# One tile as home of biases, residual, one-hots and split scores, and another first stage, in a hybrid conv, attention and PEER step

## The chip, the cores and the metric

The kernel runs on one core of one Trainium2 chip. The metric is the device time of one execution in microseconds. The kernel before took 1293.79 us in the median of three runs (1292.43 to 1293.86). The profiled execution took 1293.86 us; its span, from the first to the last recorded instruction, is 1292.1 us.

## The reference, cut to what matters

One layer over 256 prompt rows and 32 sample rows (8 sequences of 4), model width 1024, all in fp32:

```
h  = rmsnorm(x) * g1
p  = h @ w_in                        # 76 column tiles of 128: conv, q, k, v, gates
yA = w_out_a(B * conv3(C * hc))
yB = w_out_b(attention(q, k, v))     # 3 windows x 8 head slots, distance biases
x  = x + w_o(sigmoid(ga) * yA + sigmoid(gb) * yB)
h2 = rmsnorm(x) * g2
q  = h2 @ peer_wq                    # product keys, top 16 of 16 x 16
x  = x + sum over 16 experts of gate * gelu(h2 . u[e]) * v[e]
y  = rmsnorm(x) * gfin
```

The outputs are y and the updated key, value and convolution buffers. For the prompt rows all 16384 experts are computed densely and gated by one-hot products; for the 32 sample rows the chosen experts are gathered. The updated caches are mostly copies of the old ones, 56 transfers from DRAM to DRAM, most of them 1 MB.

## The kernel before, in words

The weights are 368 blocks of 128 x 1024 (`wpack`), each 0.52 MB. SP's queue loads them in order into four buffers `raw`; ACT rounds each to a high half `whi` (line 102), VectorE or, for the blocks in `pool_lo`, GpSimd subtracts for the low half `wlo` (line 103). Three splits stand ahead of the block in use. A block with eight k tiles takes 24 matmuls: high by high, high by low and low by high (`mm3`, lines 116 to 120). The blocks in order are q (0 to 11), k (12 to 23), v, conv (36 to 59), w_out_a with gate A, w_out_b with gate B (76 to 87), w_o (88 to 95), peer_wq (96 to 111), U (112 to 239) and V (240 to 367).

Every engine runs its instructions in the order in which the program writes them. A generator scheduler (`Flow`) steps attention and normalisation pieces in between the blocks of the projections. Waits are put in by the framework: an instruction waits for what wrote the parts that it reads, and a tile of a new pool waits for the tiles of the closed pools before it.

**First stage (lines 195 to 241).** Eight constant matmuls (`heat`, line 222). SP's queue gets the first slice of x transposed (`xf`, four slices of 0.29 MB), then raw0, then the other slices, then raw1 and so on. ACT's queue gets g1 and x in its natural layout (`xt`, 1.18 MB). ACT and VectorE split `xf` times g1 into `uxH` and `uxL`, eight slices of 128 x 288 (lines 232 and 233); behind slice 3 the split of block 1 stands in both queues. Blocks 0 to 2 have their low halves from GpSimd. Block 0's matmuls with the low weights come behind its others (lines 279 to 283). Three squares of `xt` on ACT give the row sums, `rstd` the reciprocal root (a dozen small operations), and three products with the identity a diagonal, which a matmul with ones spreads over the partitions behind block 3 (line 509): q is computed from unnormalised x and scaled afterwards.

**Biases.** `biasS` and `biasP` are loaded on POOL's queue behind the first stage (lines 254 and 255), with the convolution's weights and state and two K chunks behind them. The sample and prompt scores read them.

**w_o (lines 695 to 735).** Behind gate B the program issues six of the cache copies on SP (line 688), splits the first w_o block, closes the attention pools and opens new ones. POOL's queue then loads x transposed again (`x2T`, 1.18 MB, line 702), `g2T` (4 KB), `g2n` (0.52 MB) and `iotaR` (64 KB). For each of eight column tiles c: 24 matmuls into one of two accumulators, then on VectorE

```
V.tensor_add(x2T[:, c, :], x2T[:, c, :], o[:, :NT])
...
S.activation(u2H[:, c, :], x2T[:, c, :], AF.Copy, scale=g2T[:, c:c + 1])
```

then the low half `u2L`, a square on ACT and its addition to `ssum`. ACT's split of a coming weight block stands between two rounds. On SP's queue the loads of block 94 and later stand behind the six copies.

**U stage (lines 1024 to 1053).** 128 blocks of scores with gelu. In between, 64 steps build one-hot tiles `hot` and weighted ones `wgt` (lines 980 to 988, both 128 x 1024 in fp16, three buffers each), whose matmuls give the dense gates. `ev` (two buffers) holds gelus on their way to be gated.

**V stage (lines 1058 to 1080).** 128 blocks; for each pair of experts `split_w` makes high and low halves `ah` and `al` of the gated scores (128 x 512, two buffers each), a pair ahead of the matmuls. Then the final norm.

Of the kernel before, what the change touches and what calls it, by code (L numbers as in the profile page):

```python
# [19 lines left out]
P = 128  # L20
# [46 lines left out]
def emit(ctx, tc, a):  # L67
# [19 lines left out]
    pool_lo = {0, 1, 2} | set(range(B_WQ + 5, B_U + 48, 2))  # L87
# [102 lines left out]
    x2d = a["x2_spill"]  # L190
    ca = ExitStack()
    pa = ca.enter_context(tc.tile_pool(name="pa", bufs=1, side="right"))
    if True:
        with ExitStack() as c1:
            hH = p2.tile([P, KT, NT], F32R, tag="hi", name="hH")
            hL = p2.tile([P, KT, NT], F32R, tag="lo", name="hL")
            uxH = pa.tile([P, KT, 384], F32R, tag="hi", name="uxH")[:, :, :NT]
            uxL = pa.tile([P, KT, 384], F32R, tag="lo", name="uxL")[:, :, :NT]
            ss = cp.tile([P, 3], F32, name="n1s")
            with tc.tile_pool(name="pn1", bufs=1) as pn:  # L200
                xf = pn.tile([P, KT, NT], F32, name="xf")
                xt = pn.tile([P, 3, D], F32, name="xt")
                sq = pn.tile([P, D], F32, name="sq")
                g1T = pn.tile([P, KT], F32, name="g1T")
                warm = pn.tile([P, P], F32, name="warm")
                V.memset(warm, 1.0)
                V.memset(ss, 1.0)
                S.dma_start(g1T, a["g1T"])
# [5 lines left out]
                G.dma_start(cst, a["consts"][:, 128:177])  # L214
                G.dma_start(ident, a["consts"][:, 0:128])
# [3 lines left out]
                load_to(RAW)  # L219
                S.activation(ss[:1, 0:1], warm[:1, 0:1], AF.Sqrt)  # L220
                heat = bg.get()
                for _ in range(8):
                    T.matmul(heat[:, :P], warm, warm, start=True, stop=True)
                bg.put()

                def square(t):
                    w = NS if t == 2 else P
                    S.activation(sq[:w], xt[:w, t, :], AF.Square, accum_out=ss[:w, t:t + 1])

                split_next()  # L230
                for k in range(KT):
                    S.activation(uxH[:, k, :], xf[:, k, :], AF.Copy, scale=g1T[:, k:k + 1])
                    V.scalar_tensor_tensor(uxL[:, k, :], xf[:, k, :], g1T[:, k:k + 1], uxH[:, k, :].bitcast(F32),
                                           op0=OP.mult, op1=OP.subtract)
                    if k == 3:
                        split_next()
                split_next()
# [11 lines left out]
            biasP = p1.tile([P, 1152], F32, tag="bp", name="biasP")  # L249
            biasS = p1.tile([P, 1088], F32, tag="bs", name="biasS")  # L250
            convw = p1.tile([P, 8, 3], F32, name="convw")
            stT = p1.tile([P, 8, 8, 2], F32, name="stT")
            cvo = p1.tile([P, 8, 18], F32, name="cvo")
            G.dma_start(biasS, a["biasS"])
# [35 lines left out]
            def kv_load(n):  # L290
                while kv_n[0] < min(n, 28):
                    i = kv_n[0]
                    st, ch = divmod(i % 14, 7)
                    if i < 14 and i % 4 >= 2:
                        kvt[i] = pa.tile([P, 3072], F32, tag=("hi", "lo")[i % 2], name=f"kv{i}")[:, :2048]
# [183 lines left out]
            ones = p1.tile([P, P], F32, name="ones")  # L479
            rrow = wk.tile([P, NT], F32, tag="t", name="rrow", bufs=5)  # L480
            V.memset(ones, 1.0)
            for t in range(3):
                w = P if t < 2 else NS
                V.tensor_scalar_mul(diag[:w, t * P:t * P + w], ident[:w, :w], rs[:w, t:t + 1])
# [105 lines left out]
            zH = pa.tile([P, KT, 384], F32R, tag="hi", name="zH")[:, :, :NT]  # L590
            zL = pa.tile([P, KT, 384], F32R, tag="lo", name="zL")[:, :, :NT]
# [63 lines left out]
            flow.drain()  # L655

            mixH = pa.tile([P, KT, 384], F32R, tag="hi", name="mixH")[:, :, :NT]
            mixL = pa.tile([P, KT, 384], F32R, tag="lo", name="mixL")[:, :, :NT]
# [42 lines left out]
    x2T = pt2.tile([P, KT, NT], F32, name="x2T")  # L701
    G.dma_start(x2T, a["xT"])
# [240 lines left out]
    def run_s(i):  # L943
# [6 lines left out]
        if g:  # L950
            e = oh.tile([P, NP], F32, tag="ev", name=f"ev{i}", bufs=2)
# [26 lines left out]
    def gates():  # L978
        def hot(u):
            e = oh.tile([P, 2, 2, P, 2], F16, tag="hot", name=f"hot{u}", bufs=3)  # L980
# [316 lines left out]
```

## Time and profile before

| | |
|---|---|
| runs | 1292.43, 1293.79, 1293.86 us |
| profiled execution | 1293.86 us, span 1292.1 us |
| TensorE busy | 1232.3 us, 95% of the span |
| VectorE busy | 936.6 us, 72% |
| ACT busy | 592.3 us, 46% |
| GpSimd busy | 155.2 us, 12% |
| granted TensorE clock, mean | 0.983 of full |

Busy shares are means over stages with different limits, so the place where TensorE stands still is what one looks for. A wait is put down to the event that came last. Packets are what one DMA engine moved at a time; each transfer is spread over 16 engines, and each engine ends its part with a small packet that counts up a semaphore.

### The profile page before, as it was taken

To read this page: it belongs to the slowest core of one execution; us is meant where nothing else is said; L and a number is where in the kernel's file an instruction comes from. 1 tells how busy PE (TensorE), PEld (TensorE's weight loads), DVE (VectorE), ACT (ScalarE), POOL (GpSimd) and SP (SyncE) were. 2 spreads that over 40 slices of the span, in tenths; PEclk is the share of its full clock that TensorE was granted. 3 is DMA by queue.
4 is the path that set the end of the run, shared out by engine and by line. 5 is a ranking of instruction groups with operands and counts; after the bars stand their busy time and mean duration, and the time that the engine had idled before them with its cause. 6 is when DMAs were issued, how large, how long until landed. Compare 5 with 4: busy or idle time off the path is not lost.

```text
span 1292.1 us, 22943 instructions
## 1 busy us (share of the span) xinstructions
PE 1232.3 (95%) x9110; PEld 1126.9 (87%) x9110; DVE 936.6 (72%) x1720; ACT 592.3 (46%) x976; POOL 155.2 (12%) x110
## 2 busy tenths in 40 slices
PE   6999999999995799999999999999999999999996
PEld 6989998888995799989999999999988888888884
DVE  4745366764553565998997889899778877878875
ACT  4433443333352455544535444444455555555553
POOL 3000000000000022354400000000111111111100
PEclk7999999999998899999999999999999999999998
DMA  8587766566447567768767777675778888888872
GB/s 306 189 303 289 244 231 228 183 231 218 137 163 273 199 238 275 278 214 285 268 231 274 255 282 283 240 258 196 240 267 320 298 301 317 290 303 307 302 257 108
DMA packets 68235, 325.65 MB, mean 252 GB/s; under 512 B 8560, under 2 KB 8720, under 8 KB 59168
## 3 DMA queue, kind: packets, MB, share of 16 engines
q1 hardware_dynamic: 55984, 249.46, 55.5%
q0 software_dynamic: 9600, 67.19, 13.9%
q10 hardware_dynamic: 2544, 7.55, 1.5%
q8 instruction: 71, 1.16, 0.3%
q14 instruction: 36, 0.29, 0.1%
HBM read 318.19 MB, written 60.10 MB: 293 GB/s over the span
## 4 chain that ended last, share of the span: by engine, by line
PE 85%; DVE 7%; ACT 3%; DMA 3%; issue 2%; POOL 0%; DVEq 0%; SPq 0%; ACTq 0%
PE wide L1079 26%; PE acc L118 17%; PE acc L119 16%; PE acc L120 16%; DVE wlo L103 2%; PE wide L1002 2%; DMA iotaR<-iotaR 2%; ACT whi L102 2%; PE bg L356 1%; PE bg L325 1%; PE bg L444 1%; DVE tp_eq L854 1%; PE bg L390 1%; PE bg L346 1%; DVE qbd L376 1%
## 5 line engine op out<-in xcount | busy, mean ns | idle before, releaser
L103 DVE TENSOR_TENSOR wlo<-raw,whi 128x1024 fp32r<-128x1024 f32 x335 | 413.6, 1235 | 240.3 <-ACT whi L102 238.4
L102 ACT CAST whi<-raw 128x1024 fp32r<-128x1024 f32 x368 | 386.3, 1050 | 186.5 <-PE wide L1079 158.5
L120 PE MATMUL acc<-h2H,wlo 128*128 128x256 f32 x1024 | 289.4, 283 | 4.3 <-DVE wlo L103 4.0
L118 PE MATMUL acc<-h2H,whi 128*128 128x256 f32 x1024 | 292.9, 286 | 0.0
L119 PE MATMUL acc<-h2L,whi 128*128 128x256 f32 x1024 | 291.0, 284 | 0.0
L120 PEld LDWEIGHTS acc<-h2H,wlo 128*128 128x128 f32 x1024 | 193.1, 189 | 4.9 <-DVE wlo L103 4.4
L118 PEld LDWEIGHTS acc<-h2H,whi 128*128 128x128 f32 x1024 | 195.5, 191 | 0.2 <-issue 0.2
L119 PEld LDWEIGHTS acc<-h2L,whi 128*128 128x128 f32 x1024 | 194.7, 190 | 0.0
L118 PE MATMUL acc<-hH,whi 128*128 128x288 f32 x512 | 157.3, 307 | 1.9 <-ACT hH L494 1.1
L1079 PE MATMUL wide<-whi,ah 128*128 128x512 f32 x504 | 155.4, 390 | 1.6 <-ACT ah L1066 1.6
L1079 PE MATMUL wide<-wlo,ah 128*128 128x512 f32 x504 | 155.3, 389 | 0.0
L1079 PE MATMUL wide<-whi,al 128*128 128x512 f32 x504 | 155.1, 389 | 0.0
L120 PE MATMUL acc<-hH,wlo 128*128 128x288 f32 x512 | 150.8, 294 | 1.5 <-DVE wlo L103 1.5
L119 PE MATMUL acc<-hL,whi 128*128 128x288 f32 x512 | 151.2, 295 | 0.4 <-DVE hL L496 0.4
L1079 PEld LDWEIGHTS wide<-whi,ah 128*128 128x128 f32 x504 | 94.4, 188 | 22.1 <-ACT ah L1066 2.7
L1079 PEld LDWEIGHTS wide<-wlo,ah 128*128 128x128 f32 x504 | 94.6, 188 | 19.8
L1079 PEld LDWEIGHTS wide<-whi,al 128*128 128x128 f32 x504 | 94.6, 188 | 19.7
L118 PEld LDWEIGHTS acc<-hH,whi 128*128 128x128 f32 x512 | 96.0, 188 | 13.5 <-issue 8.5
L103 POOL TENSOR_TENSOR wlo<-raw,whi 128x1024 fp32r<-128x1024 f32 x33 | 83.4, 2528 | 139.8 <-ACT whi L102 133.7
L120 PEld LDWEIGHTS acc<-hH,wlo 128*128 128x128 f32 x512 | 96.3, 188 | 1.8 <-DVE wlo L103 1.8
L119 PEld LDWEIGHTS acc<-hL,whi 128*128 128x128 f32 x512 | 96.3, 188 | 0.6 <-DVE hL L496 0.6
L955 ACT ACTIVATE act<-acc 128x256 f32<-128x256 f32 (+30 forms) x124 | 40.8, 329 | 96.8 <-PE acc L120 96.5
(316 smaller groups left out, 1731.1 us busy)
## 6 DMA issues: line engine op xcount, KB each, us to landing
raw<-wpack SPq DMA_DIRECT2D x368, 512.0 KB
kvs<-cache SPq DMA_DIRECT2D x32, 1020.0 KB
kvs<-cache SPq DMA_DIRECT2D x16, 1016.0 KB
kv<-kc POOLq DMA_DIRECT2D x14, 1024.0 KB, 7.0
kv<-vc POOLq DMA_DIRECT2D x14, 1024.0 KB, 6.3
kvs<-cache SPq DMA_DIRECT2D x8, 496.0 KB
kT_out<-kT ACTq DMA_DIRECT2D x1, 1728.0 KB
v_out<-vn ACTq DMA_DIRECT2D x6, 256.0 KB
```

Of the source, the lines that this page charges most:

```text
L102: S.copy(hi, raw)
L103: (G if i in pool_lo else V).tensor_sub(lo, raw, hi.bitcast(F32))
L118: T.matmul(out, wh, xh, start=first, stop=False)
L119: T.matmul(out, wh, xl, start=False, stop=False)
L120: T.matmul(out, wl, xh, start=False, stop=last)
L325: T.matmul(dst, qT[rows, g * 4 + pr, t * P:(t + 1) * P], kT[rows, g * 4 + pr, 0:w], start=True, stop=True)
L346: T.transpose(tb[:, (j - j0) * P:(j - j0 + 1) * P], sc[:, j * P:(j + 1) * P], ident)
L356: T.matmul(o[rows, :P], vn[:, kb, g * 512 + s * HD:g * 512 + (s + 1) * HD], pt[:, j, :], start=j == 0, stop=j == nb - 1)
L376: V.tensor_copy(qb[rows, pr, :, 2 * pr + hf, :], qT[rows, g * 4 + pr, c0:c0 + 16].rearrange("p (b t) -> p b t", b=4))
L955: S.activation(dst[:, g:], o[:, g:NP], AF.Gelu)
L1002: T.matmul(full[:, jj * P:(jj + 1) * P], e[:, 1, j // 2, :, j % 2], w[:, i, j // 2, :, j % 2], start=i == 0, stop=i == 1)
L1079: T.matmul(vacc[t][:, nn], x[:, tt], w[:, nn], start=i == 0 and j == 0, stop=i == 127 and j == 2)
```

## The change

- A pool `px` with one tile of 9 KB per partition lives throughout. It is, in turn, `bias` (both bias tables), `x2T`, `hots` (one-hots, one weighted one and the gelu buffers) and `aa` (split scores).
- x is kept transposed only. `xf` takes the buffer that `hL` gets afterwards. The row sums come from eight squares of the slices of `xf` and seven additions, and three matmuls with one column of ones, behind block 2; `rstd` and the diagonal follow there.
- raw0 is loaded ahead of `xf`; the low halves of blocks 0 to 2 go to VectorE; the splits of blocks 1 and 2 stand behind all slices of x; 20 constant matmuls instead of 8.
- The bias loads wait for a memset behind the first stage's last low half.
- x2T is loaded behind gate A, ahead of the matmuls of gate B.
- Some tiles of the pool `pa` are 288 columns wide instead of 384.

```diff
-    pool_lo = {0, 1, 2} | set(range(B_WQ + 5, B_U + 48, 2))
+    pool_lo = set(range(B_WQ + 5, B_U + 48, 2))
...
+    px = ctx.enter_context(tc.tile_pool(name="px", bufs=1))
+    bias = px.tile([P, KT * NT], F32, tag="x", name="bias")
...
-                SY.dma_start(xf[:, 0:2, :], a["xT"][:, 0:2, :])
-                load_to(1)
-                for k in range(2, KT, 2):
-                    SY.dma_start(xf[:, k:k + 2, :], a["xT"][:, k:k + 2, :])
-                load_to(2)
...
-                S.dma_start(xt[:NS, 2, :], a["x_sample"])
-                S.dma_start(xt[:, 0, :], a["x_prompt"][0:P, :])
-                S.dma_start(xt[:, 1, :], a["x_prompt"][P:NP, :])
...
-                for _ in range(8):
-                    T.matmul(heat[:, :P], warm, warm, start=True, stop=True)
...
-                    if k == 3:
-                        split_next()
-                split_next()
-                square(2)
-                square(0)
-                square(1)
-                rs = rstd(cp, ss, "n1")
...
+            biasP, biasS = bias[:, 0:1152], bias[:, 1152:2240]
...
+            load_to(1)
+            for k in range(0, KT, 2):
+                SY.dma_start(xf[:, k:k + 2, :], a["xT"][:, k:k + 2, :])
...
+            for _ in range(20):
+                T.matmul(heat[:, :P], ones, ones, start=True, stop=True)
+            bg.put()
+            split_next()
+            for k in range(KT):
+                S.activation(uxH[:, k, :], xf[:, k, :], AF.Copy, scale=g1T[:, k:k + 1])
+                V.scalar_tensor_tensor(uxL[:, k, :], xf[:, k, :], g1T[:, k:k + 1], uxH[:, k, :].bitcast(F32),
+                                       op0=OP.mult, op1=OP.subtract)
+            V.memset(bias[:, 1152:1153], 0.0)
+            split_next()
+            split_next()
             G.dma_start(biasS, a["biasS"])
...
+            ssum = wk.tile([P, NT], F32, tag="t", name="ssum", bufs=5)
+            for k in range(KT):
+                q = wk.tile([P, NT], F32, tag="t", name=f"sq{k}", bufs=5) if k else ssum
+                S.activation(q, xf[:, k, :], AF.Square)
+                if k:
+                    V.tensor_add(ssum, ssum, q)
+            hL = p2.tile([P, KT, NT], F32R, tag="lo", name="hL")
...
+                    if i < 2:
+                        continue
+                    b = bg.get()
+                    for t in range(3):
+                        w = P if t < 2 else NS
+                        T.matmul(b[:w, t:t + 1], ssum[:, t * P:t * P + w], ones[:, 0:1], start=True, stop=True)
+                    V.tensor_copy(ss[:, 0:2], b[:, 0:2])
+                    V.tensor_copy(ss[:NS, 2:3], b[:NS, 2:3])
+                    bg.put()
+                    rs = rstd(cp, ss, "n1")
+                    for t in range(3):
+                        w = P if t < 2 else NS
+                        V.tensor_scalar_mul(diag[:w, t * P:t * P + w], ident[:w, :w], rs[:w, t:t + 1])
...
+            x2T = px.tile([P, KT, NT], F32, tag="x", name="x2T")
+            G.dma_start(x2T, a["xT"])
...
-    x2T = pt2.tile([P, KT, NT], F32, name="x2T")
-    G.dma_start(x2T, a["xT"])
...
-            e = oh.tile([P, NP], F32, tag="ev", name=f"ev{i}", bufs=2)
+            e = evs[:, i % 2, :]
...
+            z = u % 3
+            e = hots[:, 0:z + 2:z + 1].rearrange("p f (q i t) -> p f q i t", q=2, t=2)
+            w = (hots[:, 6:8].rearrange("p a b -> p (a b)") if z == 2 else wgts[:, z]).rearrange(
+                "p (f q i t) -> p f q i t", f=2, q=2, t=2)
...
+            V.tensor_tensor(e, iotaR[:, None, None].broadcast_to(sh),
+                            idxT[:, u].rearrange("p f (q o t) -> p f q o t", o=1, t=2).broadcast_to(sh), op=OP.is_equal)
...
+            hots = px.tile([P, 8, 512], F16, tag="x", name="hots")
+            evs = hots[:, 4:6].rearrange("p a b -> p (a b)").bitcast(F32).rearrange("p (a b) -> p a b", a=2)
...
+    aa = px.tile([P, 2, 2, 2 * NP], F32R, tag="x", name="aa")
...
-        ah = p3.tile([P, 2 * NP], F32R, tag="ah", name=f"ah{i}", bufs=2)
-        al = p3.tile([P, 2 * NP], F32R, tag="al", name=f"al{i}", bufs=2)
+        ah, al = aa[:, i // 2 % 2, 0, :], aa[:, i // 2 % 2, 1, :]
```

## Rows read from the trace of the kernel before

**Rows 1.** The page, the span in 40 slices: TensorE's busy tenths.

```profile
PE   6999999999995799999999999999999999999996
```

**Rows 2.** Waits, 400 to 430 us: who waited for whom, us, times, longest.

```profile
PE acc L118 <- DVE x2T L726: 18.5, 1, 18.5
```

**Rows 3.** The chain in order of time, first 24 us: start, us, what.

```profile
4.66 7.77 DMA raw<-wpack
```

**Rows 4.** Tile uxL (ns min/median/max, first and last start us); groups, first 60 us (busy us, mean ns).

```profile
L233 DVE SCALAR_TENSOR_TENSOR uxL<-xf,g1T,uxH x8: 506/507/2606, 7.6 to 19.1; 128x288 fp32r<-128x288 f32 x8
...
L103 DVE TENSOR_TENSOR wlo<-raw,whi 128x1024 fp32r<-128x1024 f32 x11 | 13.5, 1225 | 9.1 <-ACT whi L102 9.1
L103 POOL TENSOR_TENSOR wlo<-raw,whi 128x1024 fp32r<-128x1024 f32 x3 | 7.4, 2454 | 9.0 <-ACT whi L102 8.7 <-DMA raw<-wpack 0.3
```

**Rows 5.** TensorE's timeline, first 40 us: start us, us, instructions (heat; blocks 1 and 3 begin).

```profile
1.06 3.78 PE L223 MATMUL bg<-warm 128*128 128x128 f32 x16 [1.06 <-DVE n1s L207]
...
22.07 0.43 PE L118 MATMUL bg<-uxH,whi 128*128 128x288 f32 x1
...
28.59 0.30 PE L118 MATMUL acc<-uxH,whi 128*128 128x288 f32 x1
```

**Rows 6.** ACT's timeline, first 60 us.

```profile
6.08 1.04 ACT L102 CAST whi<-raw 128x1024 fp32r<-128x1024 f32 x1 [1.96 <-DMA raw<-wpack]
...
13.41 1.81 ACT L232 ACTIVATE uxH<-xf,g1T 128x288 fp32r<-128x288 f32 x4
```

**Rows 7.** Window 5 to 10 us (last: GB/s); POOL's queue, first 10 us: packets, MB, share.

```profile
5.00:10.00 5.00, 0.48 (x2) 0.27 (x2) 2.41 (x2) 2.87 (x5) 2.34 (x1) 0.87 1.04 389
...
q0 software_dynamic: 64, 0.09, 2.7%
```

**Rows 8.** VectorE's timeline: the second norm's row sums, and its diagonal behind the reciprocal root.

```profile
454.59 0.15 DVE L747 COPY n2s<-bh 128x3 f32<-128x3 f32 x1
...
456.70 0.48 DVE L751 TENSOR_SCALAR diag<-ident,n_r 128x128 f32<-128x128 f32 x2
```

**Rows 9.** POOL's timeline, 380 to 460 us: the first two issues behind the attention pools.

```profile
403.86 0.53 POOL L702 DMA_DIRECT2D x2T<-xT  x1 [84.18 <-PE acc L119]
404.38 0.54 POOL L704 DMA_DIRECT2D g2T<-g2T  x1
```

**Rows 10.** DMA issues, 380 to 460 us: KB, us from issue to landing.

```profile
x2T<-xT POOLq DMA_DIRECT2D x1, 1152.0 KB, 21.2
```

**Rows 11.** DMA queues, 408 to 422 us (SP's, then POOL's): packets, MB, share.

```profile
q1 hardware_dynamic: 128, 4.18, 79.8%
q0 software_dynamic: 128, 1.18, 25.2%
```

**Rows 12.** Tile biasP: its last readers, ns and first to last start us.

```profile
L333 DVE SCALAR_TENSOR_TENSOR sc<-biasP,bg x8: 405/414/417, 226.0 to 298.7; 128x256 f32<-128x256 f32 x8
```

**Rows 13.** DMA queues, 422 to 430 us: POOL's.

```profile
q0 software_dynamic: 224, 0.59, 24.1%
```

**Rows 14.** ACT's and VectorE's timelines, w_o: first u2H, the split of raw94, the last addition.

```profile
426.60 0.54 ACT L728 ACTIVATE u2H<-x2T,g2T 128x288 fp32r<-128x288 f32 x1 [24.40 <-DMA iotaR<-iotaR]
...
437.78 1.03 ACT L102 CAST whi<-raw 128x1024 fp32r<-128x1024 f32 x1
...
450.40 0.45 DVE L726 TENSOR_TENSOR x2T<-x2T,acc 128x288 f32<-128x288 f32 x1
```

**Rows 15.** Tile hot: ns, first to last start; window 700 to 915 us (third pair: VectorE).

```profile
L983 DVE TENSOR_TENSOR hot<-iotaR,idxT x64: 679/683/689, 699.0 to 910.2; 128x1024 f16<-128x1024 f16 x64
L986 DVE TENSOR_TENSOR wgt<-hot,gaT x64: 691/692/694, 699.7 to 910.9; 128x1024 f16<-128x1024 f16 x64
...
700.00:915.00 215.00, 212.13 (x2011) 208.75 (x2011) 194.81 (x310) 95.33 (x217) 0.00 (x0) 1.00 0.71 251
```

**Rows 16.** Tile ah: the two splits of a pair, ns, first to last start.

```profile
L1066 ACT CAST ah<-act x64: 611/613/619, 929.1 to 1271.3; 128x512 fp32r<-128x512 f32 x64
L1067 DVE TENSOR_TENSOR al<-act,ah x64: 672/685/691, 929.8 to 1274.1; 128x512 fp32r<-128x512 f32 x64
```

More of the change, by code (lines that the diff above doesn't have):

```diff
@@ L195, in emit @@
             hH = p2.tile([P, KT, NT], F32R, tag="hi", name="hH")
-            hL = p2.tile([P, KT, NT], F32R, tag="lo", name="hL")
-            uxH = pa.tile([P, KT, 384], F32R, tag="hi", name="uxH")[:, :, :NT]
-            uxL = pa.tile([P, KT, 384], F32R, tag="lo", name="uxL")[:, :, :NT]
+            xf = p2.tile([P, KT, NT], F32, tag="lo", name="xf")
+            uxH = pa.tile([P, KT, NT], F32R, tag="hi", name="uxH")
+            uxL = pa.tile([P, KT, NT], F32R, tag="lo", name="uxL")
             ss = cp.tile([P, 3], F32, name="n1s")
[L200 to L208, printed above, removed]
-                SY.dma_start(xf[:, 0:2, :], a["xT"][:, 0:2, :])
-                load_to(1)
-                for k in range(2, KT, 2):
-                    SY.dma_start(xf[:, k:k + 2, :], a["xT"][:, k:k + 2, :])
-                load_to(2)
-                G.dma_start(cst, a["consts"][:, 128:177])
-                G.dma_start(ident, a["consts"][:, 0:128])
-                S.dma_start(xt[:NS, 2, :], a["x_sample"])
-                S.dma_start(xt[:, 0, :], a["x_prompt"][0:P, :])
-                S.dma_start(xt[:, 1, :], a["x_prompt"][P:NP, :])
-                load_to(RAW)
-                S.activation(ss[:1, 0:1], warm[:1, 0:1], AF.Sqrt)
-                heat = bg.get()
-                for _ in range(8):
-                    T.matmul(heat[:, :P], warm, warm, start=True, stop=True)
[L224 to L228, printed above, removed]
-                split_next()
[L231 to L234, printed above, removed]
-                    if k == 3:
-                        split_next()
-                split_next()
-                square(2)
-                square(0)
-                square(1)
-                rs = rstd(cp, ss, "n1")
@@ L253, in emit @@
             cvo = p1.tile([P, 8, 18], F32, name="cvo")
+            ones = p1.tile([P, P], F32, name="ones")
+            g1T = p1.tile([P, KT], F32, name="g1T")
+            V.memset(ones, 1.0)
+            V.memset(ss, 1.0)
+            S.dma_start(g1T, a["g1T"])
+            load_to(1)
+            for k in range(0, KT, 2):
+                SY.dma_start(xf[:, k:k + 2, :], a["xT"][:, k:k + 2, :])
+            G.dma_start(cst, a["consts"][:, 128:177])
+            G.dma_start(ident, a["consts"][:, 0:128])
+            load_to(RAW)
+            S.activation(ss[:1, 0:1], ones[:1, 0:1], AF.Sqrt)
+            heat = bg.get()
+            for _ in range(20):
[9 more added lines that the diff above has]
+            split_next()
             G.dma_start(biasS, a["biasS"])
@@ L294, in kv_load @@
                     if i < 14 and i % 4 >= 2:
-                        kvt[i] = pa.tile([P, 3072], F32, tag=("hi", "lo")[i % 2], name=f"kv{i}")[:, :2048]
+                        kvt[i] = pa.tile([P, KT * NT], F32, tag=("hi", "lo")[i % 2], name=f"kv{i}")[:, :2048]
                     else:
@@ L589, in emit @@
                 flow.step()
-            zH = pa.tile([P, KT, 384], F32R, tag="hi", name="zH")[:, :, :NT]
-            zL = pa.tile([P, KT, 384], F32R, tag="lo", name="zL")[:, :, :NT]
+            zH = pa.tile([P, KT, NT], F32R, tag="hi", name="zH")
+            zL = pa.tile([P, KT, NT], F32R, tag="lo", name="zL")
             def conv(c):
@@ L979, in hot @@
         def hot(u):
-            e = oh.tile([P, 2, 2, P, 2], F16, tag="hot", name=f"hot{u}", bufs=3)
-            w = oh.tile([P, 2, 2, P, 2], F16, tag="wgt", name=f"wgt{u}", bufs=3)
-            sh = [P, 4, P, 2]
-            V.tensor_tensor(e.rearrange("p f q i t -> p (f q) i t"), iotaR[:, None].broadcast_to(sh),
-                            idxT[:, u].rearrange("p f (q o t) -> p (f q) o t", o=1, t=2).broadcast_to(sh), op=OP.is_equal)
+            z = u % 3
+            e = hots[:, 0:z + 2:z + 1].rearrange("p f (q i t) -> p f q i t", q=2, t=2)
+            w = (hots[:, 6:8].rearrange("p a b -> p (a b)") if z == 2 else wgts[:, z]).rearrange(
+                "p (f q i t) -> p f q i t", f=2, q=2, t=2)
             sh = [P, 2, 2, P, 2]
+            V.tensor_tensor(e, iotaR[:, None, None].broadcast_to(sh),
+                            idxT[:, u].rearrange("p f (q o t) -> p f q o t", o=1, t=2).broadcast_to(sh), op=OP.is_equal)
             V.tensor_tensor(w, e[:, 0:1].broadcast_to(sh),
```

12 lines of the change are left out of this document (3 added, 9 removed).

## The prediction

> **What bounds the kernel now.** I read the page first. Of its 40 slices TensorE fills 36 to 9 tenths or more; the exceptions are the first, the last and two in the middle [rows 1]. So a part of the change counts only where TensorE stands still, and the change touches two such places. In the middle, the list of waits between 400 and 430 us shows TensorE idle for 18.5 us in one piece, because both accumulators of the w_o stage wait for the addition of the residual, and that waits for x2T [rows 2]. At the start, the chain goes through the load of the second weight block, which ACT waits for with four slices of x still unsplit [rows 3], and then through VectorE's low halves of x: half of the eight took 0.507 us, but the longest 2.606, at times when GpSimd ran one of its three weight splits of 2.454 us [rows 4]. Continuous matmul work begins with block 1 at 22.07 us and then goes at (28.59 - 22.07) / 2 = 3.26 us a block, 0.136 a matmul [rows 5].
>
> **Start.** The change removes the loads of x in its natural layout, three ACT squares, GpSimd's three splits and the wait for raw1 in the middle of the x loop; it puts raw0 ahead of x on SP's queue; it adds eight squares, seven additions and three tiny matmuls behind the splits.
> - Raw0 was usable at 6.08 us [rows 6], behind one 0.29 MB slice and beside ACT's loads. All queues together moved 389 GB/s [rows 7], so without the slice it comes 0.8 us sooner; with less beside it I take 5.0 (4.5 to 6.1).
> - ACT splits it (1.04 us, to 6.05), VectorE takes its low half, now its own work (1.23, to 7.3), then eight low halves of x at the undisturbed 0.507 (4.1, to 11.4). ACT's high halves, 1.81 us for four [rows 6], run ahead of that; the last slice of x is the 1.7th MB on the queue and lands near 8.
> - Block 0 then has only its 8 matmuls with the low weights left, 8 x 0.136 = 1.1 us, so block 1 could start at 12.5. The heat must be over too: 8 of those matmuls took 3.78 us [rows 5], 20 take at most 9.45, to 10.5, and behind them a whole block 0 of 3.3 us ends at 13.8. If the clock rises during the heat it ends earlier. I take 13.0, 9.1 us sooner than 22.07.
> - The two other splits follow on VectorE (2.46, to 13.9), then the seven additions of 0.45, a size that the trace has in the addition to x2T [rows 14], with ACT's squares in between (to 17.0), then the splits of blocks 3 and 4 (to 19.5). Block 3 starts at 13.0 + 6.5 = 19.5, after three one-column matmuls that I put at 0.4 us. The copy of the sums, the reciprocal root (456.70 - 454.59 = 2.1 us) and three diagonal products (0.24 each) [rows 8] take 3.1 us beside block 3's 3.26. That cover is just enough; if it is short, the broadcast behind block 3 waits. I take 0.3, at most 1.5 us.
> - The first bias load now waits for a memset behind the low halves of x, and behind it on POOL's queue stand convw, stT and the first two K chunks. They start near 12 us; the code asks for K at block 12, and as before these loads run beside a weight stream that has four buffers of lead, so nothing is charged.
>
> Start: 9.1 - 0.4 - 0.3 = **8.4 us** gained, bounds 4.3 (heat to 10.5 and block 0 behind it at half speed, 6.6: 22.07 - 17.1 - 0.7) and 9.5.
>
> **Middle.** The tile of x2T was free only after the attention pools closed, so POOL issued its load at 403.86 and g2T right behind it [rows 9]. It took 21.2 us [rows 10]. Why: six cache copies of 1 MB had just been issued on SP. Between 408 and 422 us SP's queue moved the last four copies in 128 packets, 32 a copy: one of 65 KB and one small one on each of 16 engines; POOL's queue moved exactly the 128 rows of x2T [rows 11]. So each engine took two rows of x2T per copy, and the load lasted as long as the copies.
>
> The change loads x2T when the biases are done; their last reader ended near 299 us [rows 12], so it is there long before w_o and costs nothing. But u2H scales by g2T too, and g2T still waits for the pools: it is issued at 403.86, first in the queue, against the same copies. Now it matters how many turns it needs. In the first 10 us POOL's queue shows 64 packets for two loads of 128 rows each [rows 7], which is 2 x (16 data + 16 semaphore): short rows of one engine travel together. The 224 packets of 422 to 430 also count up only that way (16 for x2T's semaphores, 32 for g2T, 144 for g2n, 32 for iotaR) [rows 13]. So g2T needs one turn for its data and one for its semaphores. Were it 8 packets per engine, as x2T was, it would last to the end of the copies, and the sum below would be 1281 and not 1271.
>
> [...]
>
> First turn when the third copy begins (408), second behind that copy's 65 KB. In those 14 us both queues moved 5.36 MB, 383 GB/s [rows 11]; without x2T the 4.18 MB of the four copies take 10.9 us, 2.7 each, so 411, and 1.5 us until ACT sees it (half of what x2T's signal needed, next line): u2H starts at 412.5 instead of 426.60 [rows 14]. From there the loop is as before: 450.40 - 426.60 = 23.8 us to the last residual addition [rows 14], set by VectorE and ACT and not by TensorE. Bounds: 408 (no packet of POOL's queue came through earlier) and 422 (end of the copies at 419 plus 3 us: x2T's last row was through by 422 and it landed at 403.86 + 21.2 = 425.1 [rows 9 to 11]).
>
> What is late next is raw94, behind the copies on SP's queue. They end near 408 + 10.9 = 419, the block needs about 3 us beside g2n, and some 1.5 to land: 423.5. ACT split it 11.2 us after the first u2H [rows 14], that is at 423.7. So an earlier g2T gains nothing more.
>
> Middle: 426.6 - 412.5 = **14.1 us** gained, bounds 4.6 and 15.
>
> **Everything else at nothing.** The one-hots keep their sizes; hot is written with one dimension more, but wgt has that many already and takes 692 ns against 683 [rows 15]. The split scores and gelu buffers keep two halves each, and their first write waits for the last readers as it does now. The shorter tiles remove no instruction.
>
> **Sum.** The profiled execution took 1293.86 us (span 1292.1), 0.07 above the median of the three runs. 1293.86 - 8.4 - 14.1 = 1271.4: **1271 us**.
>
> **Rivals.**
> - g2T's signal waits for all copies. For: x2T's signal came 3 us after its last row, and SP's data keep being written all the time. Against: semaphore packets of every copy went through between. The gain in the middle is then 426.6 - 422 = 4.6: 1293.9 - 8.4 - 4.6 = 1281. Chance 0.2. [...]
> - The new one-hot form loses VectorE's fast 16-bit rate. Then it costs like a 1024-wide fp32 operation, 1.225 [rows 4] instead of 0.683: 64 x 0.54 = 35 us on an engine with 215 - 194.8 = 20 us free in that stretch [rows 15]. 15 us come through: 1286. Against it stands wgt. Chance 0.05.
> - **Slower:** one tile as home of several buffers makes them wait for each other. If the two halves of aa count as one tile, each of 63 later pairs of the V stage has its matmuls wait for the next pair's split, 0.613 + 0.685 [rows 16] and some 0.1 of signals: 63 x 1.4 = 88 us, so 1359. It decides as soon as one pair waits. Against it: the high halves of x are slices of one tile too, and VectorE read the first from 7.6 us on [rows 4], while ACT wrote the last four from 13.41 on [rows 6]. Chance 0.05.
> - The start doesn't do what it says: heat and a low clock eat it. With 3 us left of it: 1277. Chance 0.05.
>
> My forecast has 0.65; its own range is 1268 to 1277. For 8 in 10 the range must take in the first rival: **1264 to 1285**, with the lower end from 9.5 at the start and a middle that neither semaphore nor raw94 holds up (408: 18.6), the upper from 4.3 and 4.6. All but the slower rival and some unnamed trouble gain far over 0.2%, about what a measurement of this kernel can tell from no change: faster 0.92, same 0.02, slower 0.06.
>
> **What would show it.** Right: block 1 starts at 12.5 to 14 us, no 2.6 us low half, no GpSimd splits; x2T lands before 340; the first u2H 12 to 16 us sooner against the last gate product; g2T in at most 32 packets; hot at 0.69 us. Wrong: g2T landing with the sixth copy, ACT idle for raw94 by more than 3 us, the broadcast behind block 3 waiting over 1.5 us, or TensorE waiting for ah or hot in the later stages.

## The result, and the profile after

The changed kernel took 1272.18 us in the median of four runs (1270.41 to 1273.75), the kernel before 1293.11 beside it. The ratio is 0.9838, interval 0.9821 to 0.9855: faster by 1.6%. The forecast was 1271, range 1264 to 1285. The profiled execution took 1273.75 us, its span is 1272.0 against 1292.1.

The page, first lines and TensorE's rows in 40 slices (busy tenths, granted clock in tenths):

```profile
span 1272.0 us, 23011 instructions
...
PE   9999999999998899999999999999999999999996
...
PEclk9999999999998899999999999999999999999998
```

The dark first slice of [rows 1] is gone; the two in the middle are lighter, and not gone.

TensorE's timeline, first 24 us, answering to [rows 5]:

```profile
1.06 7.63 PE L226 MATMUL bg<-ones 128*128 128x128 f32 x40 [1.06 <-DVE n1s L215]
8.45 0.38 PE L261 MATMUL bg<-uxH,whi 128*128 128x288 f32 x1
...
12.32 0.29 PE L118 MATMUL bg<-uxH,whi 128*128 128x288 f32 x1
...
19.27 0.65 PE L493 MATMUL bg<-ones,ssum 128*128 128x1 f32 x6
19.85 0.40 PE L118 MATMUL acc<-uxH,whi 128*128 128x288 f32 x1
...
23.17 0.94 PE L506 MATMUL bg<-diag,ones 128*128 128x128 f32 x6
```

Block 1 starts at 12.32 us instead of 22.07, block 3 at 19.85 instead of 28.59, and from there to the w_o stage TensorE has only waits that it had before, five of 0.4 to 1.5 us. Why the start is shorter, ACT's timeline and the tile uxL tell (they answer to [rows 6] and [rows 4]):

```profile
4.60 1.04 ACT L102 CAST whi<-raw 128x1024 fp32r<-128x1024 f32 x1 [1.92 <-DMA raw<-wpack]
...
10.62 1.05 ACT L102 CAST whi<-raw 128x1024 fp32r<-128x1024 f32 x1 [0.20 <-DMA raw<-wpack]
```

```profile
L231 DVE SCALAR_TENSOR_TENSOR uxL<-xf,g1T,uxH x8: 509/514/520, 6.8 to 10.5; 128x288 fp32r<-128x288 f32 x8
```

Raw1 is usable at 10.6 us, against 12.4 before [rows 3], and now no slice of x stands behind it; the longest low half of x takes 0.520 us instead of 2.606. The chain in order of time (answering to [rows 3]) still goes through raw1: its load, its two halves, and the third matmul of block 1, which needs the low one. From there on blocks 1 and 2 run without a stop.

```profile
3.20 7.39 DMA raw<-wpack
10.62 1.06 ACT whi L102
11.70 1.24 DVE wlo L103
12.98 0.40 PE bg L120
```

In the middle, the list of waits from 385 to 430 us (it answers to [rows 2]), and the chain in order of time there (start, us, what):

```profile
ACT u2H L725 <- DMA g2T<-g2T: 10.2, 1, 10.2
...
PE acc L118 <- DVE x2T L723: 6.9, 2, 5.7
ACT whi L102 <- DMA raw<-wpack: 3.3, 1, 3.3
```

```profile
395.82 22.36 DMA raw<-wpack
418.26 1.06 ACT whi L102
419.34 1.23 DVE wlo L103
```

ACT's and VectorE's timelines there, the rows that answer to [rows 14]:

```profile
403.72 0.53 ACT L725 ACTIVATE u2H<-x2T,g2T 128x288 fp32r<-128x288 f32 x1 [10.18 <-DMA g2T<-g2T]
...
418.26 1.05 ACT L102 CAST whi<-raw 128x1024 fp32r<-128x1024 f32 x1 [3.29 <-DMA raw<-wpack]
...
430.88 0.45 DVE L723 TENSOR_TENSOR x2T<-x2T,acc 128x288 f32<-128x288 f32 x1
```

TensorE waits 5.7 us in one piece instead of 18.5. It waits by way of u2H for g2T; but the chain that ends last does not go through g2T. It comes through raw94, issued at 395.82 behind six cache copies.

**Where the 20.1 us of span come from.** Block 3's first matmul is 28.59 - 19.85 = 8.7 us earlier: the start. The last residual addition is 450.40 - 430.88 = 19.5 us earlier, so the middle gave 10.8. The other 0.6 lies behind it, where the first split of the V stage stands at 908.8 us against 929.1 [rows 16], 20.3 earlier.

### The profile page after: what moved, and what is told of

It is laid out like the page before. It is cut to its first block, busy times and chain, and to the rows that moved or that the text cites. A ratio compares the mean times of both kernels' runs of the same rounds, so it can differ in the third digit from the quotient of the medians.

```text
span 1272.0 us, 23011 instructions
## 1 busy us (share of the span) xinstructions
PE 1233.2 (97%) x9140; PEld 1129.3 (89%) x9140; DVE 938.8 (74%) x1732; ACT 592.4 (47%) x978; POOL 147.2 (12%) x107
## 3 DMA queue, kind: packets, MB, share of 16 engines
q0 software_dynamic: 9600, 67.19, 14.1%
## 4 chain that ended last, share of the span: by engine, by line
PE 86%; DVE 7%; ACT 2%; DMA 2%; issue 2%; SPq 1%; DVEq 0%; ACTq 0%
PE wide L1080 26%; PE acc L118 17%; PE acc L119 16%; PE acc L120 16%; PE wide L1000 2%; DVE wlo L103 2%; DMA raw<-wpack 2%; PE bg L338 1%; ACT whi L102 1%; PE bg L307 1%; PE bg L426 1%; PE bg L372 1%; DVE tp_eq L851 1%; PE bg L328 1%; DVE qbd L358 1%
## 5 line engine op out<-in xcount | busy, mean ns | idle before, releaser
L1080 PE MATMUL wide<-whi,aa 128*128 128x512 f32 x1008 | 270.0, 389 | 1.6 <-ACT aa L1067 1.6
L1080 PEld LDWEIGHTS wide<-whi,aa 128*128 128x128 f32 x1008 | 189.1, 188 | 41.8 <-ACT aa L1067 2.7
L1080 PE MATMUL wide<-wlo,aa 128*128 128x512 f32 x504 | 155.1, 389 | 0.0
L1080 PEld LDWEIGHTS wide<-wlo,aa 128*128 128x128 f32 x504 | 94.6, 188 | 19.6
L103 POOL TENSOR_TENSOR wlo<-raw,whi 128x1024 fp32r<-128x1024 f32 x30 | 76.1, 2537 | 130.8 <-ACT whi L102 123.4
L1091 POOL DMA_INDIRECT gt<-uv,eidx x32 | 48.6, 1517 | 271.0 <-DVE accS L1100 258.1
L949 ACT ACTIVATE hots<-acc 128x256 f32<-128x256 f32 (+31 forms) x65 | 18.5, 284 | 121.1 <-issue 115.7
```

The source lines that it names most:

```text
L103: (G if i in pool_lo else V).tensor_sub(lo, raw, hi.bitcast(F32))
L949: S.activation(e[:, :g], o[:, :g], AF.Gelu)
L1080: T.matmul(vacc[t][:, nn], x[:, tt], w[:, nn], start=i == 0 and j == 0, stop=i == 127 and j == 2)
L1091: G.indirect_dma_start(out=gt, out_offset=None, in_=a["uv"], in_offset=bass.IndirectOffsetOnAxis(ap=eidx[:, j:j + 1], axis=0))
```

## The experiments

Each is the changed kernel with the edit shown, timed in five rounds beside the kernel before.

**1. Eight constant matmuls.**

```diff
-            for _ in range(20):
+            for _ in range(8):
```

> Changed kernel with 8 constant matmuls instead of 20. Theory A, the longer run keeps the clock up through block 0: in the profile after, TensorE's granted clock is 1.00 from 0 to 26 us, while in the one before it fell to 0.50 behind 8 constant matmuls. With 8 they end near 4.9 us, block 0's first matmul comes near 6.1 us and its matmuls go at the pace of the low halves of x; the clock falls to 0.50 in block 0 or 1, and block 1 (3.3 us at the full clock) costs up to 6.5: about 1275.5 us (1273.5 to 1277). Theory B, block 0 keeps TensorE busy enough: the clock stays 1.00, block 1 starts at 12.3 us as now, because the last low half of x ends near 11.4 us anyway: 1272 (1271 to 1273). Theory C, the 20 matmuls themselves hold block 0 up (its first matmul is at 8.45 us): 1270 to 1271.

1271.14 us, ratio 0.9836 (0.9823 to 0.9850): not told from the changed kernel, as theory B has it; theory C's 1270 to 1271 can't be told from that either. But B's reason, a clock that stays up, is wrong: there theory A was right, and only A's price didn't come. In the table by stretch (us, busy us of TensorE, weight loads, VectorE, ACT and GpSimd, granted clock, DMA share, GB/s):

```profile
8.00:10.00 2.00, 1.98 (x9) 1.80 (x9) 2.00 (x6) 1.92 (x5) 0.00 (x0) 0.59 1.04 420
10.00:12.00 2.00, 2.00 (x11) 2.00 (x10) 1.40 (x3) 1.76 (x3) 1.51 (x3) 0.56 1.02 418
12.00:14.00 2.00, 2.00 (x17) 2.00 (x16) 1.85 (x3) 2.00 (x7) 1.65 (x4) 1.00 0.95 322
```

While block 0 ran, the granted clock fell to 0.59 from 8 to 10 us and 0.56 from 10 to 12, and block 1 still started at 12.32 us, to the hundredth as in the changed kernel. That is chance. In this execution the loads came sooner: ACT took raw1 at 9.68 us instead of 10.62, and the last low half of x ended at 10.2 instead of 11.0. From 8 to 12 us TensorE was busy all the time and set the pace itself. In the profiles of the changed kernel and of runs 6 to 12, which all have the same start, block 3 begins 9.2 us behind ACT's split of raw1; here it is 19.36 - 9.68 = 9.7. So by an estimate from these two differences the lower clock cost about 0.5 us, and the sooner loads hid it. In the times the longer run of constant matmuls brings nothing that can be told.

**2. GpSimd's three splits again.**

```diff
-    pool_lo = set(range(B_WQ + 5, B_U + 48, 2))
+    pool_lo = {0, 1, 2} | set(range(B_WQ + 5, B_U + 48, 2))
```

> Changed kernel with the low halves of weight blocks 0 to 2 on GpSimd again. Theory A, a term of the prediction: a GpSimd split of 2.45 us and VectorE's low halves of x disturb each other, some low halves of x take up to 2.6 us again, and the low half of block 1 is there at 13.5 to 14.5 us instead of near 13: block 1 starts 2 to 4 us later, total 1275 (1273.5 to 1277). Theory B, only the order of the loads and splits mattered: every low half of x stays near 0.48 us, total 1272 (1271 to 1273).

1272.46 us, 0.9846 (0.9832 to 0.9860): not told from the changed kernel. In the profile block 3 starts at 20.56 us, 0.7 later than in the changed kernel, although raw1 came sooner: counted from ACT's split of it, at 10.00, block 3 is 10.6 us behind and not 9.2. One low half of x is slow again, but the tile's row shows that they begin at 6.1 us now, ahead of any low half of weights, and so end near the same time, at 11.4 us against 11.0:

```profile
L231 DVE SCALAR_TENSOR_TENSOR uxL<-xf,g1T,uxH x8: 505/506/2291, 6.1 to 10.9; 128x288 fp32r<-128x288 f32 x8
```

The disturbance is there, and its price of some 1.4 us doesn't show in the times, so theory A holds for the mechanism and B for the time.

**3. The split of block 1 in the middle of the loop over x**, as before:

```diff
                                        op0=OP.mult, op1=OP.subtract)
+                if k == 3:
+                    split_next()
             V.memset(bias[:, 1152:1153], 0.0)
             split_next()
-            split_next()
```

> Changed kernel with the split of block 1 again behind slice 3 of x, in the middle of the loop over x; everything else of the new start stays (raw0 first, low halves on VectorE, 20 constant matmuls). Theory A, the order of the splits is the start's main term: in the profile after, raw1 was usable at 10.6 us. ACT waits for it with slices 4 to 7 unsplit, their high halves come from 11.7 to 13.5 us, VectorE puts block 1's low half (1.23) among the low halves of x and ends those near 14.5 to 15 us, block 1 starts at 15.5 to 16.5 us instead of 12.3, block 4 at 27 to 28 instead of 24.0: total 1275.5 us (1274 to 1277). Theory B, raw1 comes early enough now that nothing else stands on the queues: block 1 starts by 13.5 us, total 1271 to 1273.

1277.59 us, 0.9887 (0.9868 to 0.9906), just above theory A's range. ACT's timeline shows the wait and the four slices behind it:

```profile
10.43 1.04 ACT L102 CAST whi<-raw 128x1024 fp32r<-128x1024 f32 x1 [1.76 <-DMA raw<-wpack]
11.38 1.81 ACT L230 ACTIVATE uxH<-xf,g1T 128x288 fp32r<-128x288 f32 x4
```

TensorE waits 2.3 and 0.9 us for slices of x, its clock is 0.66 from 12 to 16 us, block 1 starts at 16.85 and block 3 at 23.82 us, 4.0 later than in the changed kernel. The median grew by 5.4, the profiled execution's span by only 1.9; the scatter between executions is of that size, and the position of block 3 is the better measure. It scatters too: with the start unchanged it lies at 19.02 us (run 10) to 20.23 (run 12), as ACT's split of raw1 comes at 9.84 to 11.06.

**4. The same, with GpSimd's splits and eight constant matmuls.** The edits of 1, 2 and 3 together.

> As the run before, and also GpSimd's three splits and 8 constant matmuls as in the kernel before (each of these two cost about nothing alone: 1271.1 and 1272.5 us). What is left of the new start is raw0 ahead of x and the loads and squares of the natural x gone. Theory A, the parts of the old start hurt together: with raw1 late in the loop, GpSimd's splits fall among the low halves of x (up to 2.3 us each) and TensorE, short of work, falls to the half clock: block 4 starts at 29 to 32 us (24.0 changed, 32.7 before), total 1277 to 1280. Theory B, they add up as measured alone: GpSimd's 1 us, the constant matmuls' 0 on top of the run before: block 4 at 28 to 29 us, total 1275 to 1277.

1279.18 us, 0.9892 (0.9874 to 0.9910): theory A. Block 3 starts at 27.26 us. The tile uxL, then TensorE's wait for it in the first 30 us, then the stretch that shows the clock:

```profile
L231 DVE SCALAR_TENSOR_TENSOR uxL<-xf,g1T,uxH x8: 503/505/2612, 5.7 to 16.1; 128x288 fp32r<-128x288 f32 x8
```

```profile
PE bg L263 <- DVE uxL L231: 5.3, 3, 1.9
```

```profile
12.00:16.00 4.00, 1.33 (x4) 0.98 (x4) 4.00 (x3) 2.76 (x7) 3.53 (x2) 0.50 0.51 166
```

**5. The same with 20 constant matmuls**, the edits of 2 and 3.

> Split of block 1 in the middle of the loop over x, GpSimd's three splits as before, but 20 constant matmuls. With 8 of them block 3 started at 27.26 us (23.82 with 20 and VectorE's low halves; 19.85 in the changed kernel), so 3.4 us belong to GpSimd's splits and the fewer constant matmuls together. Theory A, they are GpSimd's: in that run three low halves of x took up to 2.6 us and TensorE waited 5.3 us for them; block 3 at 26 to 27.3 us, total 1278 to 1279.5. Theory B, they are the clock's, which the 20 matmuls would hold up longer: block 3 at 24 to 25 us, total 1276 to 1277.5.

1280.10 us, 0.9904 (0.9886 to 0.9921), a little over theory A's time and not told from run 4, and block 3 at 26.35, inside its range: the splits on GpSimd make most of it, in part by way of the clock (0.56 from 16 to 20 us, against 0.91 in run 3). So the start can be walked back step by step by the first matmul of block 3: 19.85 changed, 23.82 with block 1's split in the loop (4.0), 26.35 with GpSimd's splits too (2.5), 27.26 with eight constant matmuls (0.9), 28.59 before. The last 1.3 belongs to what no run undid, raw0 ahead of x and the natural x gone; it, the 0.9 and the 0.7 of run 2 are no larger than the scatter of the loads. Counted from ACT's split of raw1, which takes that scatter out, block 3 stands 9.2, 13.4, 16.9 and 17.9 us behind: steps of 4.2, 3.5 and 1.0. The order in which one undoes matters: GpSimd's splits cost 1.4 alone and 3.5 beside the wait in the loop.

**6. The load of x2T put back in the text.**

```diff
             x2T = px.tile([P, KT, NT], F32, tag="x", name="x2T")
-            G.dma_start(x2T, a["xT"])
...
+    G.dma_start(x2T, a["xT"])
     g2T = pt2.tile([P, KT], F32, name="g2T")
```

> Changed kernel with the load of x2T issued where it stood before, behind the attention pools and ahead of g2T; the tile stays where it is. Theory A: the middle part of the gain is the early load alone. x2T lands 21 us after its issue near 395 us, the first u2H starts near 418 us, raw94 is no longer waited for, the last residual addition is near 441.8 us instead of 430.9: total 1283 us (1281.5 to 1284.5), and the start part (about 8.7 us against the kernel before) stays. Theory B: the gain in the middle is small and the start brings nearly all: 1272 to 1275.

1271.62 us, 0.9838 (0.9825 to 0.9852). This run told nothing of the question, as POOL's timeline shows:

```profile
311.39 0.53 POOL L699 DMA_DIRECT2D x2T<-xT  x1 [0.28 <-issue]
395.28 0.54 POOL L701 DMA_DIRECT2D g2T<-g2T  x1 [83.37 <-PE acc L119]
```

Nothing stands between the two places on POOL's queue, and a tile that is free lets the load go at once. The place in the text was never what held x2T up; its tile was.

**7. x2T in a tile of the pool behind the attention pools**, as before.

```diff
-            x2T = px.tile([P, KT, NT], F32, tag="x", name="x2T")
-            G.dma_start(x2T, a["xT"])
...
+    x2T = pt2.tile([P, KT, NT], F32, name="x2T")
+    G.dma_start(x2T, a["xT"])
     g2T = pt2.tile([P, KT], F32, name="g2T")
```

> Changed kernel with x2T again in a tile of the pool that opens behind the attention pools, as before, with its load ahead of g2T's; only this differs from the changed kernel. (An earlier run that only put the load's line back, with the tile in its lasting home, had the load issued at 311.4 us all the same, because POOL reached it at once.) Theory A, the tile's home is what the middle gained: POOL issues x2T at 395.2 us, it lands 20 to 22 us later, the first u2H starts at 416.5 to 418.5 us, raw94 is no longer waited for, the last residual addition is at 440.5 to 442.5 instead of 429 to 431: total 1282.5 us (1280.5 to 1284.5), and 10.5 us of the 21 that the change brought remain, the start. Theory B, the middle is bounded by raw94 at 417 to 418 us anyway, so that x2T costs only what it lands later than that: under 5 us, 1272 to 1277.

1283.30 us, 0.9920 (0.9902 to 0.9937): theory A. The load landed after 19.9 us, the first addition came at 415.09, and the first u2H behind that. Its row names g2T, which stood behind x2T on the queue and took 20.2 us:

```profile
x2T<-xT POOLq DMA_DIRECT2D x1, 1152.0 KB, 19.9
```

```profile
415.98 0.54 ACT L725 ACTIVATE u2H<-x2T,g2T 128x288 fp32r<-128x288 f32 x1 [22.53 <-DMA g2T<-g2T]
```

1283.30 - 1272.18 = 11.1 us are what the lasting tile brings; the last addition moved from 430.88 to 439.8, 8.9 us of them, and the rest lies behind the w_o stage.

**8. g2T loaded early**, behind x2T at 311 us.

```diff
+    g2T = cp.tile([P, KT], F32, name="g2T")
...
             G.dma_start(x2T, a["xT"])
+            G.dma_start(g2T, a["g2T"])
...
-    g2T = pt2.tile([P, KT], F32, name="g2T")
-    G.dma_start(g2T, a["g2T"])
```

> Changed kernel with g2T loaded right behind the early x2T, into a small tile that lives throughout. Theory A, behind g2T the load of raw94 is the bound: the first u2H starts near 395.8 us instead of 403.7, blocks 88 to 93 run on, then ACT waits for raw94 until about 418, as now, since the six cache copies ahead of it on SP's queue are unchanged; the addition behind raw94's split stays near 420.5 and the end of w_o does not move. TensorE's idle time only moves, to some 8 us behind block 93, and the half clock behind it may cost some us more: total 1272 to 1276. Theory B, as the prediction's sum counted it, g2T's landing sets the loop: 8 us less, 1264 (1263 to 1266).

1271.36 us, 0.9841 (0.9822 to 0.9860): theory A, just under its range, without the price of a lower clock that it left room for. ACT's timeline, the first u2H and the split of raw94:

```profile
395.56 0.54 ACT L725 ACTIVATE u2H<-x2T,g2T 128x288 fp32r<-128x288 f32 x1 [2.28 <-DVE x2T L723]
...
416.82 1.04 ACT L103 CAST whi<-raw 128x1024 fp32r<-128x1024 f32 x1 [9.98 <-DMA raw<-wpack]
```

ACT's longest wait in the stage, 10.2 us, was taken away but for 2.3, and the end of the stage stayed: the last addition at 429.4 us, where runs 1 and 6, with g2T as late as in the changed kernel, have 428.8 and 429.1. The wait for raw94 grew from 3.29 to 9.98 us. It is the copies that both waits stand for.

**9. The copies moved**, one per gate block, from 315 us on.

```diff
                 for f in range(2):
                     flow.step()
+                    copy_some(c + f < 6)
...
-            copy_some(6)
```

> Changed kernel with the six cache copies issued one per gate block between 315 and 375 us (where the DMA engines are busy 0.55 of the time) instead of all at 391 us; g2T still waits for the attention pools. Theory A, the six copies are what the middle still waits for, through g2T and through raw94: g2T lands 3 to 5 us after its issue at 395.2 us, the first u2H starts at 398.5 to 400.5 us instead of 403.7, raw94 is not waited for, the last residual addition is 23.8 us behind the first u2H, near 423 instead of 430.9 (429.1 and 429.4 in two other runs): total 1264 us (1262 to 1266.5). Theory B, the copies only move their cost (the weight stream is late between 315 and 375 us instead): 1270 to 1273.

1265.48 us, 0.9775 (0.9754 to 0.9796): theory A. g2T, issued where it was, lands in 3.0 us instead of 8.3, ACT waits for no weight block, the last addition is at 422.1.

```profile
g2T<-g2T POOLq DMA_DIRECT2D x1, 4.0 KB, 3.0
```

**10. Three of the copies moved** (`c + f < 3`, and `copy_some(3)` where the six were).

> Changed kernel with three of the six cache copies issued earlier (one per gate block) and three left where they are. Theory A, g2T's two packets per engine wait for turns behind copy packets that are already under way, whatever stands behind them, and raw94 stands behind all copies: g2T lands 7 to 9 us after its issue as now, the first u2H stays near 403.7 us, raw94 lands some 8 us earlier and is not waited for, the last addition is near 403.7 + 0.3 + 23.8 = 427.6: total 1268.5 us (1267 to 1270). Theory B, the number of copies ahead sets g2T's landing too: it lands 4 to 6 us after its issue, total 1265 to 1267.

1267.80 us, 0.9802 (0.9783 to 0.9820): theory A.

```profile
g2T<-g2T POOLq DMA_DIRECT2D x1, 4.0 KB, 8.6
```

With three copies g2T takes as long as with six, and with none 3.0 us. By itself this run doesn't tell a gap between two copies from the end of the copies: the third copy's packets ended at 400.7 to 402.8 us, and on 15 of the 16 engines g2T came behind them. The changed kernel tells it (below). Raw94 isn't waited for, and the last addition is at 426.9, 4.0 earlier, of which 0.8 come from the start.

**11. g2T early and the copies moved**, the edits of 8 and 9.

> Both: g2T loaded right behind x2T near 312 us, and the six cache copies one per gate block. In the run with g2T early alone ACT waited 10.0 us for raw94. Theory A: that wait goes, the loop runs 3.47 us a round from the first u2H at 395.6 us, the last residual addition is near 395 + 7 x 3.47 = 419.3 us, 10 us earlier than in that run, and TensorE's clock doesn't fall before the second norm: total 1261 us (1259.5 to 1263). Theory B, as for the copies alone: they only move their cost, 1270 to 1273.

1259.30 us, 0.9733 (0.9714 to 0.9752): theory A and a hair below its range, 12.9 us better than the changed kernel. The last addition is at 419.7 us. All idle time of TensorE for the residual is gone; the loop's round of 3.47 us is what is left.

**12. The same, with the coming split ahead of u2H.**

```diff
         V.tensor_add(x2T[:, c, :], x2T[:, c, :], o[:, :NT])
         acc.put()
+        if c < 7:
+            split_ahead(B_WO + c + 1)
```

> g2T early and the copies moved, and in the w_o loop the split of the coming weight block put right behind the residual addition, ahead of u2H, u2L and the square. Theory A: the round of 3.46 us is a cycle of ACT and VectorE (addition 0.38, u2H 0.42, square 0.43, high half 0.95, low half 1.23, and the next addition stands behind that low half on VectorE); with the split first, the addition no longer waits for u2H and the square of the round before, and the round is TensorE's 24 x 0.1335 = 3.2 us: the last addition 395.3 + 7 x 3.2 = 417.8 us instead of 419.7, total 1257.5 us (1256 to 1259.5). Theory B: what the loop saves returns behind it, as u2H and u2L of the last column tiles are later: 1259 to 1261.

1258.62 us, 0.9735 (0.9718 to 0.9751). In the profile the round is 3.2 us as theory A has it (the residual additions of the tile x2T), 1.7 us less in the stage:

```profile
L723 DVE TENSOR_TENSOR x2T<-x2T,acc x8: 454/454/454, 395.6 to 418.0; 128x288 f32<-128x288 f32 x8
```

In the time it doesn't show: the two intervals are nearly the same. The clock is a candidate, argued only: of the five runs of 11, four had a mean clock of 0.996 or 0.997, all five of 12 had 0.994 or 0.995. Whether the gain is real stays open. Runs 11 and 12 both beat the changed kernel.

## Why the prediction was right, and where a term was not

**Start, predicted 8.4, measured 8.7.** Raw0 was usable at 4.60 us (predicted 5.0), VectorE's first low half stood between 5.68 and 6.9 (to 7.3), the eighth low half of x ended at 11.0 (11.4), block 1 came at 12.32 (12.5 possible, 13.0 taken). The constant matmuls ended at 8.69, inside the bound of 10.5: the first 8 take 3.78 us (run 1), the other 12 took 3.85. The three tiny matmuls and what lies round them took 19.85 - 19.27 = 0.58 (0.4), and the broadcast followed block 3 without the wait of 0.3. The reasons hold too: the wait for raw1 inside the loop is the largest part (4.0, run 3), the splits on GpSimd the next (2.5 beside it, run 5).

That the sum hit so closely is in part luck, for it gave raw1 no time of landing. In the trace raw1's split (10.62 to 11.68) and its low half (to 12.94) come last, and not the low halves of x. Block 1 stopped after two matmuls until 12.98, and blocks 1 and 2 took 19.27 - 12.32 = 6.95 us instead of 6.5. This 0.45 and the 0.2 of the tiny matmuls were made up by block 1, 0.7 before 13.0, and by the broadcast.

On GpSimd's splits the trace of the kernel before bears the prediction out one by one: they began at 7.21, 13.58 and 16.23 us, three low halves of x began 0.37 to 0.39 us behind them and took 2.28, 2.28 and 2.61 us, and the other five took 0.51. Why a low half of x takes longer beside a split of GpSimd, no run shows.

**Middle, predicted 14.1, measured 10.8.** The first u2H was predicted 8.6 us behind g2T's issue and came 403.72 - 395.21 = 8.5 behind it. The time is right; of the reason, one half. That g2T slips through between the copies holds: it landed at 403.5, and the last copy's packets ended at 413.7. That it needs a turn for its data and another for its semaphores does not hold: the turns at 408 and behind 411 were the author's estimate from counts of packets [rows 7, 11 and 13], and no run shows the second. The trace has each DMA packet with its start and its length. On each of the 16 engines the 256 bytes of g2T's data are followed within 0.01 us by the 4 bytes that count up the semaphore, and only then by the next copy's 65 KB. Both went in one gap between two copies' packets, as two rows of x2T had [rows 11].

What the 8.5 us are made of is this. Nothing of g2T moved before 399.4 us, 4.2 behind its issue. Five engines had it then, behind their packet of the second copy. On the other eleven that packet had ended by 399.1, and g2T came only behind the third copy's, at 401.6 to 402.2. One gap, on most engines a copy later than the first turn predicted, ends where the second turn would have: that is luck. Why nothing of g2T moved in the gap at 399.1, 3.9 us behind the issue, stays open; without copies (run 9) all of it had landed 3.0 us behind the issue.

Until 403.6, just behind the landing, POOL's queue had moved 42 packets and 0.05 MB, that is g2T's 32 and ten rows of g2n (4 KB each). Had it gone in eight rows per engine as x2T did, two in each gap [rows 11], it would, by an estimate from that count, have lasted to the end of the last copy. And x2T itself, issued at 311.3, landed 7.9 us later with the copies not yet there.

The failed step is "ACT split it 11.2 us after the first u2H, that is at 423.7", against raw94 at 423.5: no wait was charged. In the changed kernel's time (8.7 earlier) that is 414.8 for raw94 and 415.0 for ACT. ACT was ready at 418.26 - 3.29 = 414.97; raw94 came 3.3 us later. The term that was mis-sized is the end of the copies, 408 + 10.9 = 419, here 410.3: their last packets ended at 412.05 to 413.67 us. From there the step's 3 us and 1.5 to land were right, it took 418.26 - 413.67 = 4.6. The 10.9 came from 5.36 MB in 14 us [rows 11]. But a window of this view holds the packets that start in it, and holds them whole, as SP's row from 395 to 403.6 us (packets, MB, share) shows by its share of more than 100%:

```profile
q1 hardware_dynamic: 96, 3.13, 102.7%
```

A copy's packet lasts 2.4 to 3.5 us, so in the kernel before the last copy ended at 424.6 and not at 422. The same 5.36 MB from 408.5 to 424.6 would have given the four copies 12.6 us. They took 13.4, from 400.22, where the last engine begins the third, to 413.67, with rows of g2n between them, which the step had behind the copies. The 23.8 us from the first u2H to the last addition became 27.16 by the 3.29 of this wait; without it the loop was as predicted, 23.87.

The sentence on it, "an earlier g2T gains nothing more", was right, and more so than the sum: run 8 shows that raw94 bounds the stage whatever g2T does. The sum counted from g2T and hit only because the two ends lay 3 us apart.

**Everything else at nothing.** Hot takes 682 ns in its new form (683 before, 0.69 predicted), and TensorE's one wait for a split score in the V stage is 1.6 us, as before. The rivals of a one-hot at 1.225 us and of the tile whose halves wait for each other are out by the row of the one-hots and by TensorE's waits from 909 us on:

```profile
L982 DVE TENSOR_TENSOR hots<-iotaR,idxT x64: 677/682/693, 679.4 to 890.1; 128x1024 f16<-128x1024 f16 x64
```

```profile
PE wide L1080 <- ACT aa L1067: 1.6, 1, 1.6
```

**The rival that g2T's signal waits for all copies** (1281) is out: it landed at 403.5 while copies ran on to 413.7. What spoke for it, x2T's signal 3 us behind its last row, doesn't need it: in the kernel before x2T's last row began at 421.4 us, and its 4-byte packets begin at 422.9, where the sixth copy's packets begin to end. The rival that the start doesn't do what it says is out by block 1 at 12.32.

The sum against the profiled execution: 1271.4, plus 3.3 for raw94, less 0.3 at the start and 0.6 behind w_o, is 1273.8; it took 1273.75. The lower end of the range, 1264, isn't what its terms give: 1293.86 - 9.5 - 18.6 = 1265.8.

## What to carry to other kernels

When a chain names one late load, ask what stands ahead of it on the DMA engines, and which other load stands behind the same thing: here x2T, g2T and raw94 were all late by the same six copies, and each one taken away uncovered the next, until the copies went (1272.2 to 1265.5, with g2T early 1259.3). A load's place in the program says little if its queue is idle there (run 6 issued x2T's at 311.39 us from its later line); what its buffer waits for decides, so give what is needed right behind a stage boundary a buffer that lives across it. In a loop of loads and splits, let nothing that is already there stand in an engine's queue behind something that is not (4.0 us of block 3's start in run 3). Before a rate or an end of transfers is taken from a window of packets, add how long the last of them lasts: with packets of 3 us that was the wait that the sum missed.

## What the runs showed that was not expected

- g2T's 4 KB took 8.3 us to land beside six copies from DRAM to DRAM, 8.6 beside three (run 10) and 3.0 without (run 9). In the changed kernel its data and its semaphore passed each engine within 0.01 us of each other, between two packets of 65 KB.
- The new start hangs on the loads: in eight profiles block 3 begins 9.2 us behind ACT's split of raw1, which waits for raw1 in seven of them and lies anywhere from 9.84 to 11.06 us. A granted clock of 0.59 and 0.56 from 8 to 12 us, in block 0 of run 1, cost about 0.5 us by the estimate there, and block 1 at 12.32 us with 8 and with 20 constant matmuls hid it.
- Executions of one kernel scatter by more than some of its terms: run 11 took 1257.6 to 1263.86 us, and the longest of the five was also the only one with a mean clock of 0.992 instead of 0.996 or 0.997. In its profile the second norm shows it, TensorE's clock at 0.51 there:

```profile
425.00:430.00 5.00, 5.00 (x23) 5.00 (x23) 2.56 (x9) 0.47 (x1) 0.00 (x0) 0.51 0.89 329
```
